# State-space parameters beside the first layer: loads on GpSimd's queue, later stores, one table per piece, zeros stored first

## The chip, the cores and the metric

The kernel runs on one core of one Trainium2 chip. The metric is the device time of one execution in microseconds; lower is better. TensorE is the engine for matrix products, VectorE, ScalarE and GpSimd are the engines for elementwise work, and SyncE only issues transfers. In the rows of the profile they are PE (PEld is its weight load), DVE, ACT, POOL and SP; ACTq and SPq are transfers issued from ScalarE's and SyncE's queues.

## The reference

A network of four layers over 512 tokens and 2048 channels in float32: "ab" (gated linear attention and forgetting attention), "c" (a state space layer, S5), then an even and an odd layer. Each ends with a projection added to its input. What the change touches is the preparation of layer c's parameters, which depend on the weights alone:

```python
step = jnp.exp(log_step)[:, None]
mag = jnp.exp(lr * step)
lb_re, lb_im = mag * jnp.cos(li * step), mag * jnp.sin(li * step)
den = lr * lr + li * li
nr, ni = lb_re - 1.0, lb_im
coef_re = (nr * lr + ni * li) / den
coef_im = (ni * lr - nr * li) / den
bb_re = coef_re[..., None] * b_re - coef_im[..., None] * b_im
bb_im = coef_re[..., None] * b_im + coef_im[..., None] * b_re
...
# x_t = Lbar x_{t-1} + Bbar u_t ; y_t = Re(C x_t) + D u_t
```

Groups of 16 channels share a state of 64 complex numbers. The kernel evaluates the recurrence in chunks, so it needs tables of powers of Lbar, and products of B and C with such powers.

## The kernel before

Every large product is taken over float32 values that are split in a high and a low part, with three matmuls for each product of two values. A weight tile of 128 x 512 is loaded by SyncE's queue into `wraw` (3 buffers); ScalarE writes its high part and VectorE its low part into `whl` (4 buffers); TensorE then does 12 matmuls of 512 columns with it, into `pj`. This repeats all through the kernel: one tile after another, with the attention, gates and norms of the layers in between. So ScalarE and VectorE have to be in time with one split each per tile.

The parameters of layer c are made beside layer ab. `emit` defines `params(o)`, and layer ab calls it as `beside(o)` at 21 places ("pieces"): 0 before the forgetting attention, 1 to 8 in its loop, 9 to 12 after the gates, 13 to 20 behind the chunks of the first `w_out` (line 480). Piece 0 is `s5_params`: chains of small rows on GpSimd that make the powers and store them per batch in DRAM (`s5tab`, lines 988 to 992), and `s5w`. There are 16 batches of S5 groups, and for each of them two more things are made:

- `s5_tables`, two batches in each of the pieces 1 to 8: a load of `lm` from `s5tab` (line 1004), four multiplications and two sums on VectorE (`cst`, `acc`, `hc`), and two stores on ScalarE's queue (lines 1020 and 1021).
- `s5_batch_params`, one batch in each of the pieces 3 to 18: loads of `smb`, `s5_bc` and `s5w` on SyncE's queue (lines 1032, 1040, 1041), a scale of -C on ScalarE (line 1043), products on GpSimd into two `hc` tiles that are cleared first and stored (lines 1052 and 1060), GG on VectorE (six rows, `vs` and `acc`) with a store on ScalarE, and BB on GpSimd (`fac`). At the next piece the second half follows: 16 small matmuls into `tr`, placed behind the last matmul so far (`net.last`), X3 from them, and four small stores (line 1093).

The order of the instructions on each engine comes from a planner that puts rows where it expects their inputs to be ready; `after(...)` puts a row behind a given one. Each engine works its rows in order. A tag of tiles has a fixed number of buffers: `acc`, `cst`, `fac` and `lm` have one, `hc` and `vs` four, `rawb` eight. A row that needs a buffer waits until the earlier user of it is done. `acc` is also the sum of squares that `w_out` gathers for the next norm.

## Time and profile before

| | |
|---|---|
| median of 3 runs | 3410.19 us (3409.04 to 3414.12) |
| the profiled execution | 3407.61 us |
| its span, first to last instruction | 3405.8 us |
| mean granted clock of TensorE | 0.994 |
| GpSimd busy | 23 % of the span |
| transfers | 390 MB |

The profile is of one execution. Its span leaves 1.8 us outside. The granted clock is a share of full speed. The rows below are its views: the page, tables by windows of time, sums of waits, groups of equal instructions, and the timeline.

### The profile page before, as it was taken

What the parts mean: (1) busy time and instruction counts of PE and PEld (TensorE: products, weight loads), DVE (VectorE), ACT (ScalarE), POOL (GpSimd) and SP (SyncE); (2) the same over time, 40 slices, a digit from 0 to 9 for tenths busy, and PEclk for the clock granted to TensorE, in tenths of its full rate; (3) what the DMA queues carried; (4) which work ended last, traced back from release to release, by engine and by line L of the source; (5) the groups of instructions that cost most, each with busy time, mean ns of one, the idle gap of its engine ahead of it and who ended that gap; (6) DMA issues with size and microseconds to landing.
All of it is one profiled execution on the core that took longest, in us unless ns stands there. A gap on an engine that the chain in (4) does not pass through costs nothing.

```text
span 3405.8 us, 45778 instructions
## 1 busy us (share of the span) xinstructions
PE 3349.1 (98%) x16332; PEld 2722.4 (80%) x16332; DVE 1907.8 (56%) x3213; ACT 1337.7 (39%) x2497; POOL 784.1 (23%) x974
## 2 busy tenths in 40 slices
PE   9999999999999999999999999999999999999997
PEld 8888776777788888888888777888888788888885
DVE  5753457787556576834354655453544545647634
ACT  5443432233343333423343655232433444535532
POOL 0330364348602223200221100012110120212011
PEclk9999999999999999999999999999999999999999
DMA  5223335576634444343443223334333223332343
GB/s 156 72 69 91 87 109 159 169 218 207 206 107 132 135 144 141 116 121 118 145 127 90 66 75 90 94 120 145 105 92 81 73 65 81 80 88 75 106 120 106
DMA packets 389013, 390.01 MB, mean 115 GB/s; under 512 B 66968, under 2 KB 327448, under 8 KB 388784
## 3 DMA queue, kind: packets, MB, share of 16 engines
q1 hardware_dynamic: 362992, 354.64, 36.4%
q10 hardware_dynamic: 22464, 22.12, 1.9%
q0 software_dynamic: 3328, 10.32, 0.8%
q8 instruction: 128, 2.10, 0.3%
q14 instruction: 101, 0.83, 0.1%
HBM read 340.71 MB, written 46.25 MB: 114 GB/s over the span
## 4 chain that ended last, share of the span: by engine, by line
PE 73%; DVE 2%; POOL 1%; issue 1%; DMA 0%; DVEq 0%; ACT 0%; SPq 0%
PE pj L152 66%; PE sc L152 3%; PE po L152 3%; PE tr L156 1%; POOL wt L140 1%; DVE wk L140 0%; PE tr L152 0%; DVE hl L140 0%; DMA vs<-s5w 0%; DVE wk L1139 0%; DVE whl L140 0%; POOL cst L140 0%; DVE ha L143 0%; DVE sc L140 0%; DVE hc L143 0%
## 5 line engine op out<-in xcount | busy, mean ns | idle before, releaser
L152 PE MATMUL pj<-hl,whl 128*128 128x512 f32 x10224 | 2459.6, 398 | 14.8 <-DVE whl L140 7.3
L152 PEld LDWEIGHTS pj<-hl,whl 128*128 128x128 f32 x10224 | 1912.8, 189 | 456.3 <-DVE whl L140 10.2
L140 DVE TENSOR_TENSOR whl<-wraw,whl 128x512 fp32r<-128x512 f32 (+2 forms) x1064 | 805.3, 759 | 1082.7 <-ACT whl L137 1077.5
L137 ACT ACTIVATE whl<-wraw 128x512 fp32r<-128x512 f32 (+2 forms) x1064 | 661.5, 623 | 1353.9 <-PE pj L152 1096.6
L152 PE MATMUL pj<-whl,hl 128*128 128x512 f32 (+2 forms) x2112 | 466.1, 380 | 4.1 <-DVE whl L140 2.3
L152 PEld LDWEIGHTS pj<-whl,hl 128*128 128x128 f32 x2112 | 375.4, 191 | 81.4 <-DVE whl L140 3.1
L140 POOL TENSOR_TENSOR acc<-acc,wt 128x512 f32<-128x512 f32 x73 | 102.7, 1415 | 798.7 <-ACT wt L137 797.4
L137 ACT ACTIVATE wk<-sc,sm 128x256 f32<-128x256 f32 (+3 forms) x160 | 79.6, 502 | 90.3 <-DVE sm L148 86.8
L140 POOL TENSOR_TENSOR ha<-wk,ha 64x512 fp32r<-64x512 f32 x32 | 45.0, 1407 | 290.7 <-ACT ha L137 264.2
L140 POOL TENSOR_TENSOR wt<-wt,acc 64x508 f32<-64x508 f32 x32 | 63.9, 1995 | 181.4 <-DVE wt L140 125.7
L140 POOL TENSOR_TENSOR wt<-ha,wk 128x256 f32<-128x256 f32 x72 | 61.9, 888 | 127.4 <-PE sc L152 66.9
L152 PE MATMUL po<-pt,vs 128*128 128x128 f32 x560 | 80.0, 276 | 0.2
L152 PEld LDWEIGHTS po<-pt,vs 128*128 128x128 f32 x560 | 72.8, 192 | 3.2 <-ACT pt L137 0.8
L152 PE MATMUL sc<-ha,ha 128*128 128x128 f32 (+1 forms) x224 | 71.2, 390 | 3.5 <-DVE ha L140 2.7
L156 PE MATMUL tr<-ident,wk 128*128 128x128 f32 x416 | 71.4, 275 | 1.4 <-DVE pt L509 1.1
L137 ACT ACTIVATE pt<-tr 128x384 f32<-128x384 f32 (+3 forms) x96 | 46.7, 486 | 62.0 <-PE tr L156 60.1
L148 DVE TENSOR_SCALAR wk<-wk,sm 128x256 f32<-128x256 f32 (+3 forms) x160 | 65.4, 422 | 4.5
L140 POOL TENSOR_TENSOR fac<-wt,acc 128x512 fp32r<-128x512 f32 x8 | 10.8, 1353 | 244.3 <-ACT acc L137 130.3
L156 PEld LDWEIGHTS tr<-ident,wk 128*128 128x128 f32 x416 | 52.0, 141 | 18.8 <-issue 3.4
L137 ACT ACTIVATE ge<-ge 128x512 f32<-128x512 f32 x64 | 40.3, 630 | 66.7 <-DVE ge L140 55.7
L521 DVE TENSOR_REDUCE sm<-sc 128x1 f32<-128x128 f32 (+3 forms) x96 | 45.8, 487 | 34.1 <-PE sc L152 33.5
L140 POOL TENSOR_TENSOR cst<-vs,vs 128x256 f32<-128x256 f32 x64 | 53.5, 855 | 32.1 <-DMA vs<-s5w 18.8
(316 smaller groups left out, 2984.3 us busy)
## 6 DMA issues: line engine op xcount, KB each, us to landing
wraw<-in_l_w_in_dram SPq DMA_DIRECT2D x272, 256.0 KB, 2.8
wraw<-in_ab_w_in_dram SPq DMA_DIRECT2D x216, 256.0 KB, 2.8
wraw<-in_c_w_in_dram SPq DMA_DIRECT2D x128, 256.0 KB, 2.7
wraw<-in_l_w_out_dram SPq DMA_DIRECT2D x128, 256.0 KB, 2.9
wraw<-in_ab_w_out_dram SPq DMA_DIRECT2D x64, 256.0 KB, 3.4
wraw<-in_glu_w_dram SPq DMA_DIRECT2D x64, 256.0 KB, 2.9
wraw<-in_c_w_out_dram SPq DMA_DIRECT2D x64, 256.0 KB, 3.0
wraw<-in_l_w_in_dram SPq DMA_DIRECT2D x128, 128.0 KB, 2.3
```

The costliest lines, as they stand in the source:

```text
L137: return self.nc.scalar.activation(out, in_, func, **kw)
L140: return (eng or self.nc.vector).tensor_tensor(out, a, b, op=op)
L148: return e.tensor_scalar(out, a, s1, None, op0=op0)
L152: return self.nc.tensor.matmul(out, l, r, start=start, stop=stop)
L156: return self.nc.tensor.transpose(out, in_, self.ident[:k, :k])
L521: self.nc.vector.tensor_reduce(mx, pb[:, 0:w], axis=AX.X, op=ALU.max)
```

## The change

It moves and re-cuts the making of the parameters; what is computed stays the same.

- The loads of `s5_tables` and `s5_batch_params` go from SyncE's queue to GpSimd's. `s5_bc` is loaded in two parts, the part with C into a tile that all batches share by halves (`small`).
- `s5_tables` makes one batch per piece, in pieces 1 to 16, each of its rows behind VectorE's last two-operand row so far (`last_dve`). Its stores come a piece later, behind ScalarE's last row so far (`last_act`).
- The store of GG, and those of X3, come a piece later than their data.
- The products of B are no longer put into cleared tiles. `s5_clear`, in pieces 0 to 3, stores zeros over the whole of the 16 targets in DRAM (16 stores of 512 KB on ScalarE's queue), and each batch stores its 128-partition product in two strided stores of 512 pieces of 256 B (GpSimd's queue). 
- The scale of -C goes from ScalarE to GpSimd, a copy of X3 from ScalarE to VectorE.
- Other buffers: the power tables in `rawb` in place of `vs`, `wrow` in `lm` in place of `ha`, BB in two halves of one `fac` tile, GG in turn in `acc2` and `hc`, the products in `bc`.

```diff
     def act(self, out, in_, func=AF.Copy, **kw):
-        return self.nc.scalar.activation(out, in_, func, **kw)
+        self.last_act = self.nc.scalar.activation(out, in_, func, **kw)
+        return self.last_act
...
-    def s5_tables(self, b0):
+    def s5_tables(self, b):
...
-        tab = self.t("lm", [P, S])[:, 0:384].rearrange("p (b f) -> p b f", b=2)
-        self.dma.dma_start(tab, self.s5tab[b0:b0 + 2, :, 0:192].rearrange("b p f -> p b f"))
-        for b in range(2):
...
+        tab = self.t("lm", [P, S])
+        nc.gpsimd.dma_start(tab[:, 0:192], self.s5tab[b][:, 0:192])
...
+        with self.after([self.last_dve]):
             self.tt(v4(u[0]), av(0), bv(0), A.mult)
...
-            d = self.dp.tile([P, 2, S], F32, name=self.name("s5ph"))
+        yield
+        d = self.dp.tile([P, 2, S], F32, name=self.name("s5ph"))
+        with self.after([self.last_act]):
             nc.scalar.dma_start(d[:, 0], C)
             nc.scalar.dma_start(d[:, 1], Sn)
...
     def s5_batch_params(self, b):
...
-        self.dma.dma_start(M, self.s5tab[b][:, 196:236])
+        if b == 0:
+            self.s5bb = self.t("fac", [P, 2, 2, 4, 32])
+            self.s5small = self.t("hc", [P, 2, 256])
+        BB, small = self.s5bb[:, b % 2], self.s5small[:, b % 2]
+        CP, X3 = small[:, 0:128].rearrange("p (i q c) -> p i q c", i=2, q=4), small[:, 128:240]
+        g.dma_start(M, self.s5tab[b][:, 196:236])
...
-        self.dma.dma_start(X1[:, 0:896], I["s5_bc"][b])
-        self.dma.dma_start(Y[:, 0:512],
-                           self.wtab[b].rearrange("g s i q p -> (g s) (i q p)").unsqueeze(1).to_broadcast([8, 16, 512]))
-        self.act(X1[:, 320:384], X1[:, 320:384], scale=-1.0)
+        g.dma_start(X1[:, 0:768], I["s5_bc"][b][:, 0:768])
+        g.dma_start(small[:, 0:128], I["s5_bc"][b][:, 768:896])
+        g.dma_start(Y[:, 0:512],
+                    self.wtab[b].rearrange("g s i q p -> (g s) (i q p)").unsqueeze(1).to_broadcast([8, 16, 512]))
+        self.ts(small[:, 64:128], small[:, 64:128], -1.0, eng=g)
+        g.memset(X3[:, 0:48], 0.0)
...
         for i in range(2):
-            o = self.hd("hc")
-            g.memset(o, 0.0)
-            self.tt(z0, BT[:, 0], WT[:, i], A.mult, eng=g)
+            self.tt(o[:, i], BT[:, 0], WT[:, i], A.mult, eng=g)
             self.tt(z1, BT[:, 1], WT[:, 1 - i], A.mult, eng=g)
-            for gg in range(2):
-                r = slice(64 * gg, 64 * gg + 64)
-                self.tt(o[r].rearrange("p (q g f) -> p q g f", q=4, g=2)[:, :, gg],
-                        z0[r].rearrange("p (q f) -> p q f", q=4), z1[r].rearrange("p (q f) -> p q f", q=4),
-                        A.add if i else A.subtract, eng=g)
-            g.dma_start(d[1][:, i], o)
+            self.tt(o[:, i], o[:, i], z1, A.add if i else A.subtract, eng=g)
+        for gg in range(2):
+            r = slice(64 * gg, 64 * gg + 64)
+            g.dma_start(d[1][r].rearrange("p i (q g f) -> p (i q) g f", q=4, g=2)[:, :, gg],
+                        o[r].rearrange("p i (q f) -> p (i q) f", q=4))
...
+    def s5_clear(self, batches):
+
+        zero = self.t("rawb", [P, S])
+        self.nc.gpsimd.memset(zero, 0.0)
+        for b in batches:
+            d = [self.dp.tile(sh, F32, name=self.name("s5d")) for sh in ([P, 2, 256], [P, 2, S], [4, P, 64])]
+            self.s5d.append(d)
+            with self.after([self.last_act]):
+                self.nc.scalar.dma_start(d[1], zero.unsqueeze(1).to_broadcast([P, 2, S]))
...
             if o == 0:
                 net.s5_params()
-            elif o <= 8:
-                net.s5_tables(2 * (o - 1))
-            for b in pending:
-                with net.after([net.last]):
-                    next(b, None)
-            pending.clear()
+            if o < 4:
+                net.s5_clear(range(4 * o, 4 * o + 4))
+            for b in list(pending):
+                if next(b, b) is b:
+                    pending.remove(b)
+            if 1 <= o <= 16:
+                pending.append(net.s5_tables(o - 1))
+                next(pending[-1])
             if 3 <= o < 19:
                 pending.append(net.s5_batch_params(o - 3))
-                next(pending[0])
+                next(pending[-1])
```

What this does to the order of the rows on two engines is seen at three places. `whl` is a weight split; the numbers are those of the tiles. The code's lines are moved by the change: line 1020 of before is 1029, 140 is 142, 143 is 148.

First place: ScalarE's order in the forgetting attention, with the phase table stores (lines 1020 and 1021, `s5ph`), a store's data being VectorE's `hc`. Before:

```order
L137 ACTIVATE rawb_4220<-po_4209 128x512
L137 ACTIVATE whl_4637<-wraw_4635 128x512
L1020 DMA s5ph_4058<-hc_4048 128x512
L137 ACTIVATE vs_4252<-vs_4252 128x64
L137 ACTIVATE whl_4654<-wraw_4652 128x512
L1021 DMA s5ph_4058<-hc_4049 128x512
L137 ACTIVATE whl_4671<-wraw_4669 128x512
L1020 DMA s5ph_4071<-hc_4061 128x512
L137 ACTIVATE whl_4688<-wraw_4686 128x512
L1021 DMA s5ph_4071<-hc_4062 128x512
```

In the change, at the same head's end:

```order
L138 ACTIVATE rawb_4279<-po_4268 128x512
L1029 DMA s5ph_4299<-hc_4123 128x512
L1118 DMA s5d_4284<-rawb_4281 256x1x512
L1118 DMA s5d_4288<-rawb_4281 256x1x512
L1118 DMA s5d_4292<-rawb_4281 256x1x512
L138 ACTIVATE whl_4711<-wraw_4709 128x512
L1118 DMA s5d_4296<-rawb_4281 256x1x512
L1030 DMA s5ph_4299<-hc_4124 128x512
L138 ACTIVATE whl_4728<-wraw_4726 128x512
L138 ACTIVATE whl_4745<-wraw_4743 128x512
```

The stores between weight splits have become those of the table of a piece before (`hc_4123` beside piece tiles numbered over 4270), and the zero stores (line 1118) stand among them.

Second place: VectorE's order in the gates, from the 226th weight tile to the 227th or 228th; `lm` is a table's load, `ge` a gate, `hl` the split of `w_out`'s input. Before:

```order
L140 TENSOR_TENSOR whl_6863<-wraw_6861,whl_6863 128x512
L143 SCALAR_TENSOR_TENSOR vs_6162<-own,cols,tr_6350 128x16
L140 TENSOR_TENSOR whl_6880<-wraw_6878,whl_6880 128x512
L140 TENSOR_TENSOR acc_6399<-vs_6377 128x256
L140 TENSOR_TENSOR ge_6760<-pj_6628,bc_230 128x512
L140 TENSOR_TENSOR vs_6377<-vs_6376,smb_6374 128x256 x2
L140 TENSOR_TENSOR acc_6399<-vs_6377 128x256
L140 TENSOR_TENSOR vs_6591<-vs_6590,smb_6588 128x256 x2
L140 TENSOR_TENSOR whl_6897<-wraw_6895,whl_6897 128x512
```

In the change:

```order
L142 TENSOR_TENSOR whl_6824<-wraw_6822,whl_6824 128x512
L142 TENSOR_TENSOR hc_6103<-cst_6104,acc_6105 128x512
L142 TENSOR_TENSOR hc_6130<-vs_6115 128x256
L148 SCALAR_TENSOR_TENSOR rawb_4279<-ge_6509,rawb_4279 128x512
L142 TENSOR_TENSOR acc_6350<-vs_6335 128x256
L142 TENSOR_TENSOR whl_6841<-wraw_6839,whl_6841 128x512
L142 TENSOR_TENSOR vs_6115<-hc_4316,smb_6112 128x256 x2
L142 TENSOR_TENSOR ge_6715<-pj_6583,bc_230 128x512
L142 TENSOR_TENSOR cst_6324<-lm_6320 128x512
L142 TENSOR_TENSOR acc_6325<-lm_6320 128x512
L142 TENSOR_TENSOR hc_6130<-vs_6115 128x256
L142 TENSOR_TENSOR whl_6858<-wraw_6856,whl_6858 128x512
```

Table rows (`cst`, `acc` from `lm`, and `hc`) now stand between the weight splits here, beside GG's rows; before, all tables were done by this place.

Third place: VectorE's order in the first tiles of layer c, the 305th to the 307th. Before, three weight splits stood in a row (`whl_8988`, `whl_9005`, `whl_9022`), with nothing between them up to the 313th:

```order
L140 TENSOR_TENSOR whl_8988<-wraw_8986,whl_8988 128x512
L140 TENSOR_TENSOR whl_9005<-wraw_9003,whl_9005 128x512
L140 TENSOR_TENSOR whl_9022<-wraw_9020,whl_9022 128x512
L140 TENSOR_TENSOR whl_9039<-wraw_9037,whl_9039 128x512
L140 TENSOR_TENSOR whl_9056<-wraw_9054,whl_9056 128x512
```

In the change:

```order
L142 TENSOR_TENSOR whl_8968<-wraw_8966,whl_8968 128x512
L142 TENSOR_TENSOR hc_7481<-cst_7483,acc_7484 128x512
L142 TENSOR_TENSOR cst_7483<-lm_7479 128x512
L142 TENSOR_TENSOR acc_7484<-lm_7479 128x512
L142 TENSOR_TENSOR whl_8985<-wraw_8983,whl_8985 128x512
L142 TENSOR_TENSOR hc_7482<-cst_7483,acc_7484 128x512
L142 TENSOR_TENSOR hc_7509<-vs_7494 128x256
L142 TENSOR_TENSOR vs_7494<-hc_4316,smb_7491 128x256 x2
L142 TENSOR_TENSOR hc_7509<-vs_7494 128x256
L142 TENSOR_TENSOR whl_9002<-wraw_9000,whl_9002 128x512
```

The tables of the last batches stand here, behind the norm that frees `acc`, and the rows of GG that go with them.

## Rows read from the trace of the kernel before

**Rows 1.** The page's first part: busy us (share of the span) x instructions, by engine.

```profile
PE 3349.1 (98%) x16332; PEld 2722.4 (80%) x16332; DVE 1907.8 (56%) x3213; ACT 1337.7 (39%) x2497; POOL 784.1 (23%) x974
```

**Rows 2.** Windows: stretch, length, busy PE, PEld, DVE, ACT, POOL, clock, DMA share, GB/s.

```profile
500.00:550.00 50.00, 39.63 (x148) 29.42 (x148) 41.80 (x53) 8.44 (x16) 38.79 (x89) 0.86 0.61 180
...
660.00:700.00 40.00, 36.55 (x188) 27.81 (x187) 35.56 (x69) 10.87 (x27) 21.80 (x31) 0.96 0.76 212
...
760.00:810.00 50.00, 41.74 (x249) 31.28 (x248) 47.46 (x62) 16.91 (x35) 43.67 (x63) 0.93 0.55 171
```

**Rows 3.** Waits of TensorE, 420 to 1000: total us, times, longest.

```profile
PE pj L152 <- DVE whl L140: 9.6, 7, 3.6
PE tr L152 <- POOL fac L140: 7.0, 5, 5.4
```

**Rows 4.** Waits of ScalarE, 500 to 560 us.

```profile
ACT whl L137 <- DVE hc L140: 29.7, 9, 5.7
```

**Rows 5.** Timeline, 500 to 526: start, us, instruction, idle before and its releaser.

```profile
505.74 0.33 ACTq L1021 DMA_DIRECT2D s5ph<-hc  x1
...
506.19 0.63 ACT L137 ACTIVATE whl<-wraw 128x512 fp32r<-128x512 f32 x1 [5.66 <-DVE hc L140]
...
509.37 1.06 DVE L140 TENSOR_TENSOR cst<-lm 128x512 f32<-128x512 f32 x1 [3.66 <-DMA lm<-s5tab]
...
512.07 13.16 PE L152 MATMUL pj<-hl,whl 128*128 128x512 f32 x48 [3.58 <-DVE whl L140]
```

**Rows 6.** Chain of waits, 770 to 802: start, us, what.

```profile
793.10 3.97 DMA vs<-s5w
...
800.47 0.44 PE tr L152 x24
```

**Rows 7.** Waits of SyncE's queue, 440 to 900 us.

```profile
SPq L1041 <- DVE acc L140: 19.5, 8, 4.3
```

**Rows 8.** Groups of VectorE, 440 to 1000: busy us, mean ns, idle before.

```profile
L140 DVE TENSOR_TENSOR whl<-wraw,whl 128x512 fp32r<-128x512 f32 x170 | 140.4, 831 | 114.0 <-ACT whl L137 113.5
L140 DVE TENSOR_TENSOR vs<-vs,smb 128x256 f32<-128x256 f32 x64 | 42.9, 708 | 6.3 <-POOL cst L140 2.0 <-POOL wt L988 1.8 <-DMA s5d<-vs 1.4
...
L140 DVE TENSOR_TENSOR cst<-lm 128x512 f32<-128x512 f32 x32 | 35.2, 1099 | 19.3 <-DMA lm<-s5tab 10.9 <-POOL hc L140 8.3
L140 DVE TENSOR_TENSOR hc<-cst,acc 128x512 f32<-128x512 f32 x32 | 22.2, 694 | 0.5
L140 DVE TENSOR_TENSOR acc<-vs 128x256 f32<-128x256 f32 x32 | 20.0, 624 | 1.7 <-DMA s5d<-acc 1.3
...
L140 DVE TENSOR_TENSOR hl<-rawb,hl 128x512 fp32r<-128x512 f32 x8 | 6.4, 822 | 1.8 <-ACT hl L137 1.8
```

**Rows 9.** TensorE's `pj` matmuls alone in a full stretch: busy us, count, clock.

```profile
850.00:1000.00 150.00, 146.55 (x621) 1.00 0.53 165
```

**Rows 10.** Groups of GpSimd, 440 to 1000.

```profile
L140 POOL TENSOR_TENSOR hc<-cst 64x256 f32<-64x256 f32 x64 | 56.5, 883 | 3.5
L140 POOL TENSOR_TENSOR cst<-vs,vs 128x256 f32<-128x256 f32 x64 | 53.5, 855 | 32.1 <-DMA vs<-s5w 18.8 <-DVE sm L148 5.9 <-DVE hc L140 4.0
...
L1060 POOL DMA_DIRECT2D s5d<-hc x32 | 18.6, 580 | 4.5 <-POOL hc L140 4.5
L1052 POOL MEMSET hc<- 128x512 f32 x32 | 16.7, 525 | 40.0 <-DMA s5ph<-hc 19.2 <-DMA s5d<-hc 9.0 <-DVE sm L530 7.6
```

**Rows 11.** Timeline of GpSimd and VectorE, 499 to 513.

```profile
500.49 1.13 DVE L140 TENSOR_TENSOR acc<-lm 128x512 f32<-128x512 f32 x1
...
500.63 1.08 POOL L989 COPY wt<-hc 128x32 f32<-128x32 f32 x1
...
502.40 1.07 POOL L992 DMA_DIRECT2D s5tab<-wt  x2
...
502.93 1.07 DVE L140 TENSOR_TENSOR cst<-lm 128x512 f32<-128x512 f32 x1
...
505.80 0.21 POOL L989 COPY wt<-hc 128x32 f32<-128x32 f32 x1
```

More of the change, by code (lines that the diff above doesn't have):

```diff
@@ L112, in __init__ @@
         self.dma = nc.sync
+        self.s5d = []
         self.setup()
@@ L946, in s5_params @@
         cmul(N[11], N[12], c2, d2, c2, d2)
-        Tb = [self.t("vs", [P, 16, H]) for _ in range(2)]
+        half = lambda: self.hd("rawb").rearrange("p (n h) -> p n h", h=H)
+        Tb, Tb2 = [half(), half()], [half(), half()]
         Ta = [self.t("hc", [P, 8, H]) for _ in range(2)]
@@ L1080, in s5_batch_params @@
+            self.tt(v1, BP[:, 1], co(1 - i), A.mult, eng=g)
+            self.tt(BB[:, i], v0, v1, A.add if i else A.subtract, eng=g)
         yield
+        with self.after([self.last_act]):
+            nc.scalar.dma_start(d[0], GG)
         pt = self.ps("tr")
         rows = lambda q: slice(32 * q, 32 * q + 32)
-        for i in range(2):
-            for q in range(4):
-                self.mm(pt[rows(q), 0:16], BB[:, i, q], CP[:, i, q], start=(i == 0), stop=(i == 1))
-        for i in range(2):
-            for q in range(4):
-                self.mm(pt[rows(q), 16:64], BB[:, i, q], GG[:, i, q * 64:q * 64 + 48], start=(i == 0), stop=(i == 1))
@@ L1089, in s5_batch_params @@
-        g.memset(X3[:, 0:48], 0.0)
-        self.stt(X3[:, 48:64], self.own, self.c("s5_d", b), pt[:, 0:16], A.mult, A.add)
-        self.act(X3[:, 64:112], pt[:, 16:64])
-        for s_ in range(4):
-            nc.scalar.dma_start(d[2][s_], X3[:, 48 - 16 * s_:112 - 16 * s_])
+        with self.after([self.last]):
+            for i in range(2):
+                for q in range(4):
+                    self.mm(pt[rows(q), 0:16], BB[:, i, q], CP[:, i, q], start=(i == 0), stop=(i == 1))
+            for i in range(2):
+                for q in range(4):
+                    self.mm(pt[rows(q), 16:64], BB[:, i, q], GG[:, i, q * 64:q * 64 + 48], start=(i == 0), stop=(i == 1))
@@ new lines, in s5_batch_params @@
+        with self.after([self.last_dve]):
+            self.stt(X3[:, 48:64], self.own, self.c("s5_d", b), pt[:, 0:16], A.mult, A.add)
+            nc.vector.tensor_copy(X3[:, 64:112], pt[:, 16:64])
+        yield
+        with self.after([self.last_act]):
+            for s_ in range(4):
+                nc.scalar.dma_start(d[2][s_], X3[:, 48 - 16 * s_:112 - 16 * s_])
+    def s5_clear(self, batches):
[4 more added lines that the diff above has]
+            self.s5d.append(d)
+            with self.after([self.last_act]):
+                self.nc.scalar.dma_start(d[1], zero.unsqueeze(1).to_broadcast([P, 2, S]))
@@ L1610, in emit @@
                 net.s5_params()
+                net.s5_clear(range(16))
                 for b in range(16):
-                    if b % 2 == 0:
-                        net.s5_tables(b)
+                    for _ in net.s5_tables(b):
+                        pass
                     for _ in net.s5_batch_params(b):
```

58 lines of the change are left out of this document (29 added, 29 removed).

## The prediction

> **What bounds the kernel now.** I read the page's busy times first: TensorE is busy for 98 per cent of a span of 3405.8 us [rows 1], so a change can only move the few stretches in which TensorE stands still or runs at a lower clock. The table by windows shows where these lie: in 420 to 1000 us, where the S5 parameters are made beside the first layer, there are three. Stage A, 500 to 550 us, has 39.63 us of TensorE in 50 at a granted clock of 0.86; stage B, 660 to 700, has 36.55 in 40 at 0.96; stage C, 760 to 810, has 41.74 in 50 at 0.93 [rows 2]. So 10.4, 3.5 and 8.3 us are idle. A granted clock under 1.00 is a mixture of the levels 2.4 and 1.2 GHz, and the three stretches that idle are the three with a lower one; what it costs is busy time by what is missing to 1.00: 5.5, 1.5 and 2.9 us. All that these parameters cost today is thus 15.9 + 5.0 + 11.2 = **32 us**. No edit to them can give more.
>
> The waits then say who ended the idling. TensorE's two largest are for VectorE's low half of a weight tile (9.6 us) and for GpSimd's `fac` (7.0) [rows 3]. They are two mechanisms. In stage A, ScalarE waited 29.7 us in nine pieces for VectorE's `hc` ahead of a weight split [rows 4]. The timeline shows one: the store of a phase table (L1021) is issued at 505.74, just after VectorE made it, and the weight split behind it on ScalarE's queue had stood 5.66 us. VectorE itself then waits 3.66 us for the next table's load, with a weight split behind that row, and TensorE starts 3.58 us late at 512.07 [rows 5]. In stage C it is the chain of a batch: a load of 3.97 us, GpSimd's multiplications, its `fac`, and only then TensorE's small matmuls [rows 6].
>
> **The change, part by part.** *Stage A.* The stores move a piece later, so their data are old when ScalarE comes to them (the order's first place). One table per piece, not two, halves VectorE's burst. Also SyncE no longer stands in front of the weights with parameter loads: its largest such stand, L1041 for VectorE's `acc`, is 19.5 us [rows 7]. I take the whole 15.9 us as gone. Bounds: 12 if the tables still left there cost the 3.66 us of one load wait, 15.9 if not.
>
> *Stage B.* Nothing new stands there and VectorE does less; I take the 5.0 as gone; bounds 0 and 5.0.
>
> *Stage C.* The batch chain's cost, 11.2 us, goes only if nothing takes its place. But a table per piece takes sixteen pieces, and the gates and the first w_out chunks now carry them. I count VectorE's rows in the new order between the 221st and the 248th weight tile: 23 table multiplications at 1.099 us (25.3), 12 table sums at 0.694 (8.3), 22 and 10 for GG at 0.708 and 0.624 (15.6 and 6.2), 28 weight splits at 0.831 (23.3) and 32 rows of gates and `hl` splits, all taken at the 0.822 of `hl` (26.3): **105 us** [rows 8]. TensorE has 28 tiles of 12 matmuls there. A stretch with nothing between them has 621 in 146.55 us [rows 9], so 0.236 each and 79 us. Before, the same tiles had no table rows: 23.3 + 17.0 + 7.5 for GG + 24.7 for 30 others = 72 us, under TensorE's 79. The excess of 26 us is softened by the four `whl` buffers, 4 x 12 x 0.236 = 11.3 us of lead if they are full. So about 14.5 us idle. With the clock on top, which cost 0.53 us per idle us in stage A and 0.35 in C, I take 0.44: **+21**. Bounds: 9 if gaps elsewhere on VectorE's list let it catch up by a further 5 us and the clock holds; 26 x 1.53 = 40 if no lead exists.
>
> *Start of layer C.* The table's `acc` has one buffer, which w_out's sum of squares holds until the norm. So the tables of the last batches leave w_out and stand in layer C's first tiles (the order's third place). Between tiles 302 and 316, VectorE has 15 splits (12.5), 15 multiplications (16.5), 8 sums (5.6), 14 and 8 for GG (9.9 and 5.0) and 2 rows of the norm (1.6): 51 us, against 182 matmuls, 43 us; before, 14 us. The excess is 8. Bounds: 0 with the lead full, 8 x 1.53 = 12 with none. I take the middle, **+6**: the rows just ahead are the `hl` splits, which leave little lead.
>
> *Zeros.* Sixteen stores of 512 KB stand in ScalarE's order, behind GpSimd's memsets. The trace has no such wait. The lower bound is 0, since a full lead covers three tiles, 8.5 us. The upper is stage A's, a ScalarE wait of 5.66 us that made TensorE 3.58 us late, for two of them: 7. I take **+2**, nearer to 0, because the memsets need only `rawb`.
>
> *GpSimd.* Its queue gets five load issues per batch: 80 at 0.580 us (a batch's store; 46 us). It loses 32 memsets at 0.525 (17) and 64 half adds at 0.883 (57), and gets 32 full ones at 0.855 (27) [rows 10]: about 0 in sum. The two stores of 512 short pieces have no row; I take the 0.580 of a store of 128 rows as the lower bound and four times that as the upper, 1.7 us more each, and take the lower. The scale of -C and the copy of X3 change engines; they are one short row each per batch, beside TensorE's tiles, and without that cover 16 times no more than the 0.21 to 1.08 us of a small copy [rows 11]. The zeros' 8 MB go beside the weights, at DMA shares of 0.55 to 0.76 [rows 2], and I cost them at nothing; if the weights came late by them, it would show as ScalarE waiting for `wraw`.
>
> Here the trace speaks on GpSimd and VectorE together: a 32-column copy took 1.08 us beside a table row of VectorE and 0.21 without one, while a pair of DMA issues took 1.07 us beside such a row [rows 11]. So copies are held and issues are not; the sum goes by the rows, with 0.58 us per issue, and an issue that is held as the copy was is a rival below. The Trainium skill (SBUF — State Buffer, section "SBUF: two separate sides", the box on DMAs issued from GpSimd) says that VectorE can lock GpSimd out of a port pair that they share, that a DMA on GpSimd's queue then can't get its descriptors, and that ScalarE's or SyncE's queue should be taken instead; it gives about 0.62 us alone and 3.1 us overlapped. By it, as an estimate from that page, the 80 loads would take up to 2.5 us more each, 200 us of GpSimd's time, and the sum would be that of the rival or worse. The copies here agree with it, the issue rows do not.
>
> *Sum:* -15.9 - 5.0 - 11.2 + 21 + 6 + 2 = -3, so 3407.6 becomes about 3405 for an execution like the profiled one. That one lies 2.6 us under the median of the runs shown, 3410.19. So **3407 us**. About 0.2 per cent, 6.8 us, is what a measurement of this kernel can tell from no change.
>
> **Rivals.** *All hidden.* VectorE's list has gaps that my count does not see (it idles in 44 per cent of the span [rows 1]), the lead stays and the new rows cost a few us. Stages A to C give back 32 less up to 9, so -23 to -32: 3378 to 3387, say 3384. For it: before, tables beside attention cost nothing outside three stretches. Against it: the 105 against 79.
>
> *Slower, VectorE binds twice.* It is the mechanism of stage C without a lead, and layer C's likewise: -32 + 40 + 12 + 2 = +22, so 3432. It decides when VectorE's rows per tile stay above TensorE's 2.83 us for longer than four tiles; for it, stage A lost 10.4 us in just such a stretch [rows 2]; against it, part of that came from ScalarE's stores, which are mended, and VectorE's list there had the load wait besides.
>
> *Slower, GpSimd's queue is late.* If each of a batch's seven or eight issues is held for a table row, 1.1 us, then GpSimd needs 8 us more per batch; its chain already ended the wait in stage C [rows 6]. The four batches whose tables stand in layer C's first tiles have 43 us there; 32 us late there, less the lead of 11, with the clock 30: 3407.6 + 30 + 2.6 = 3440. The equal 1.07 us of issues speak against it [rows 11]. By that page's rule it would be the likeliest.
>
> *Not done as said:* if the stores still stood ahead of their data, nothing would change in stage A: 3410 + 13 = 3423; the order excludes it for the rows shown.
>
> **Numbers.** Forecast (the costs move from stages A and B to stage C and layer C, 3397 to 3417): 0.45. All hidden: 0.26. VectorE twice: 0.20, with the undone case. GpSimd's queue: 0.09. The forecast's own spread lies by 0.10 below and 0.05 above the 0.2 per cent. So faster 0.36, the same 0.30, slower 0.34. The range leaves out the worst of the slower cases and the last of the hidden one: 3380 to 3434.
>
> **What would show it.** Right: no ScalarE wait for `hc` ahead of a weight split near 500 to 560 us and that stretch full; TensorE waiting for VectorE's `whl` near 770 to 830, with VectorE at ten tenths; tables' rows beside layer C's first matmuls. Wrong: stage A still with waits, stage C full in spite of the tables (all hidden), VectorE waiting for `lm` while GpSimd's issues last longer than 0.6 us (its queue), or a wait of ScalarE for `rawb` near 400 or 450.

## The result and the profile after

| | before | after |
|---|---|---|
| median | 3410.89 us (4 runs) | 3435.2 us (3430.44 to 3436.57, 4 runs) |
| the profiled execution, its span | 3407.61, 3405.8 us | 3430.44, 3428.6 us |
| mean granted clock of TensorE | 0.994 | 0.993 |

The ratio is 1.0069, 95% interval [1.0057, 1.0081]: slower, by 0.7 per cent. The forecast was 3407 in 3380 to 3434; the median lies 1.2 us over the range, next to the rival in which VectorE binds twice (3432). The profiled execution of the changed kernel is the fastest of its four, 4.8 us under their median.

The table by windows of the changed kernel, columns as in [rows 2], shows where the idling went:

```profile
380.00:420.00 40.00, 35.66 (x156) 26.19 (x156) 25.65 (x58) 12.72 (x30) 37.49 (x71) 1.00 0.49 151
...
460.00:500.00 40.00, 37.80 (x179) 29.39 (x178) 24.52 (x59) 15.25 (x36) 22.01 (x56) 1.00 0.65 202
500.00:550.00 50.00, 50.00 (x229) 40.94 (x229) 16.80 (x27) 12.33 (x20) 3.08 (x7) 1.00 0.48 145
...
660.00:700.00 40.00, 40.00 (x190) 31.72 (x189) 30.74 (x78) 15.04 (x35) 15.67 (x23) 1.00 0.63 173
700.00:760.00 60.00, 55.83 (x333) 44.13 (x332) 39.52 (x58) 18.02 (x31) 31.38 (x35) 0.97 0.61 177
760.00:810.00 50.00, 39.90 (x209) 29.09 (x207) 42.68 (x61) 13.62 (x24) 42.41 (x44) 0.93 0.50 145
810.00:830.00 20.00, 11.61 (x72) 8.79 (x72) 13.61 (x20) 2.30 (x4) 18.06 (x28) 0.74 0.61 164
830.00:900.00 70.00, 66.39 (x349) 52.78 (x350) 42.02 (x55) 19.34 (x31) 48.42 (x69) 0.98 0.71 217
...
1000.00:1040.00 40.00, 33.23 (x205) 25.11 (x204) 31.50 (x51) 5.58 (x9) 25.43 (x34) 0.91 0.63 180
1040.00:1100.00 60.00, 57.28 (x343) 47.04 (x342) 37.57 (x62) 24.13 (x47) 22.40 (x32) 1.00 0.47 137
```

Stages A and B of [rows 2] are full. In 700 to 900 us TensorE now idles for 4.2, 10.1, 8.4 and 3.6 us; with the clock's share (busy time by what is missing to 1.00: 1.7, 2.8, 3.0, 1.3) that is 35 us. Layer C's start loses 12: 6.8 idle and 3.0 of clock to 1040, then 2.7 idle where the kernel before had 0.4. And 4.3 and 2.2 us are new at 380 to 420 and 460 to 500. The stretches in which TensorE had idled again have the lower clocks: 0.74 at 810 to 830, between the levels of 2.4 and 1.2 GHz.

TensorE's waits, 380 to 1100 us, which answer to [rows 3]:

```profile
PE pj L157 <- DVE hl L142: 9.3, 1, 9.3
PE pj L157 <- DVE whl L142: 9.1, 6, 4.3
PE tr L157 <- DVE hc L142: 7.7, 5, 2.7
PE tr L157 <- DVE hc L1104: 5.5, 2, 4.4
```

The four largest are all for VectorE. ScalarE's wait for `hc` at 500 to 560 [rows 4] is gone; its largest wait there is now for TensorE:

```profile
ACT whl L138 <- PE pj L157: 38.2, 18, 5.4
```

The longest wait of TensorE is the one to read. The timeline of the changed kernel, rows of GpSimd, VectorE and TensorE:

```profile
797.12 10.16 POOL L142 TENSOR_TENSOR vs<-vs,vs 128x256 f32<-128x256 f32 x1
807.24 0.74 POOL L142 TENSOR_TENSOR bc<-vs,vs 128x256 f32<-128x256 f32 x1
...
796.47 0.69 DVE L142 TENSOR_TENSOR ge<-pj,bc 128x512 f32<-128x512 f32 x1
797.07 1.08 DVE L142 TENSOR_TENSOR cst<-lm 128x512 f32<-128x512 f32 x1
...
805.61 1.06 DVE L142 TENSOR_TENSOR acc<-lm 128x512 f32<-128x512 f32 x1
815.36 0.47 DVE L142 TENSOR_TENSOR vs<-hc,smb 128x256 f32<-128x256 f32 x1 [8.69 <-POOL fac L142]
...
817.50 4.71 PE L157 MATMUL pj<-hl,whl 128*128 128x512 f32 x13 [9.26 <-DVE hl L142]
```

A GpSimd product that took 0.86 us on average before [rows 10] lasts 10.16 us. From 797.07 to 806.67 VectorE works without a pause, on rows that take both operands from SBUF; GpSimd's row ends 0.6 us after VectorE stops. The rest of GpSimd's batch (the next product takes 0.74) then comes late, VectorE stands 8.69 us for it with weight splits behind the waiting row, and TensorE idles 9.26 us. By these times VectorE first keeps GpSimd out, and then waits for what it kept back.

VectorE's two largest waits of this kind at 700 to 900 us; in the kernel before, none for GpSimd or for a load is over 1.3 us there:

```profile
DVE vs L142 <- DMA hc<-in_s_bc_dram: 9.6, 3, 4.6
DVE vs L142 <- POOL fac L142: 8.7, 1, 8.7
```

The row that waited 8.69 us reads C from `hc`. GpSimd issued a load of C at 813.08, after the held product, and such a load lands 2.2 us later in the median, so at about 815.3. Whether `fac` or that load let the row go can't be told from this; both stand behind the held product in GpSimd's order.

Groups of GpSimd, 400 to 1050 us, against [rows 10]:

```profile
L142 POOL TENSOR_TENSOR vs<-vs,vs 128x256 f32<-128x256 f32 x32 | 45.0, 1407 | 0.5
L142 POOL TENSOR_TENSOR bc<-vs,vs 128x256 f32<-128x256 f32 x32 | 36.2, 1133 | 30.2 <-DMA vs<-s5w 25.4 <-issue 3.8 <-DMA s5d<-bc 1.0
...
L1071 POOL DMA_DIRECT2D s5d<-bc x32 | 22.4, 708 | 3.9 <-POOL bc L142 2.6 <-issue 1.1 <-POOL hc L1059 0.2
...
L1011 POOL DMA_DIRECT2D lm<-s5tab x16 | 9.2, 577 | 68.0 <-DVE acc L142 66.0 <-DVE tk L142 2.0
```

The issues are near the forecast's 0.58 us: 0.577 for a table's load and 0.708 for a store in short pieces. The products, 64 of them at 0.855 before, now cost 1.407 and 1.133.

### The profile page after: what moved, and what is told of

It is laid out like the page before. It is cut to its first block, busy times and chain, and to the rows that moved or that the text cites. A ratio compares the mean times of both kernels' runs of the same rounds, so it can differ in the third digit from the quotient of the medians.

```text
span 3428.6 us, 45810 instructions
## 1 busy us (share of the span) xinstructions
PE 3352.5 (98%) x16332; PEld 2720.7 (79%) x16332; DVE 1895.7 (55%) x3229; ACT 1334.1 (39%) x2465; POOL 824.6 (24%) x1042
## 4 chain that ended last, share of the span: by engine, by line
PE 88%; POOL 5%; DVE 3%; DMA 2%; issue 1%; ACT 0%; DVEq 0%; ACTq 0%; SPq 0%; POOLq 0%
PE pj L157 78%; PE sc L157 5%; PE po L157 3%; PE tr L161 1%; POOL vs L142 1%; POOL wt L142 1%; PE tr L157 1%; POOL fac L142 1%; DMA vs<-s5w 0%; DVE whl L142 0%; DVE hl L142 0%; DVE acc L142 0%; POOL acc L142 0%; DMA lm<-s5tab 0%; DVE wk L142 0%
## 5 line engine op out<-in xcount | busy, mean ns | idle before, releaser
L148 DVE SCALAR_TENSOR_TENSOR ge<-ge,ge 128x512 f32<-128x512 f32 x60 | 48.9, 816 | 19.5 <-ACT ge L138 19.3
```

The source lines that it names most:

```text
L148: return self.nc.vector.scalar_tensor_tensor(out, a, s, b, op0=op0, op1=op1, **kw)
```

## The experiments

Each kernel is the changed one with the edit shown, unless it says otherwise; times stand beside the kernel before on the same chip. The loss of the change is 0.69 per cent (ratio 1.0069).

### What it is not: the queue of the loads, the zeros

**e2_loads_sp**

```diff
-        nc.gpsimd.dma_start(tab[:, 0:192], self.s5tab[b][:, 0:192])
+        self.dma.dma_start(tab[:, 0:192], self.s5tab[b][:, 0:192])
...
-        g.dma_start(M, self.s5tab[b][:, 196:236])
+        self.dma.dma_start(M, self.s5tab[b][:, 196:236])
```

(and the three others of a batch.)

> The change with one part undone: the five loads of a batch (table, smb, two of s5_bc, s5w) are issued from SyncE's queue again; tables, stores and zeros stay as changed. Theory A expects no large move, 3427 to 3440, with long rows on GpSimd near 750 and 800 still there. Theory B expects most of the loss back, 3400 to 3415.

3429.88 us, ratio 1.0059 [1.0046, 1.0073]. The loads' queue comes out at 0.1 per cent, which the intervals do not tell from nothing. Long GpSimd products stay: the longest lasts 7.9 us. In the windows of the one profiled execution two moves offset each other: 700 to 900 loses 28 us where the changed kernel loses 35, and 460 to 500 loses 8.9 where it loses 2.2.

**e3_zeros_first**

```diff
-            if o < 4:
-                net.s5_clear(range(4 * o, 4 * o + 4))
...
+            net.s5_clear(range(16))
             h = net.layer_ab(raws, beside=params if "c" in layers else None)
```

> The change with the 16 zero stores moved to the start of the kernel, ahead of layer ab, in place of pieces 0 to 3. If the zeros and their memsets cost the 6.5 us of idle TensorE in 380 to 420 and 460 to 500, 3426 to 3431; if that idling is of GpSimd's power chains and not of the zeros, 3433 to 3437. Theories A and B say the same of the rest: 700 to 900 stays as it is.

3446.3 us, 1.0108 [1.0094, 1.0122], above both ranges: in 0 to 100 us TensorE is busy for 83.26 us, where the kernel before has 93.70. But the idling that the edit was to remove is still there, 3.6 of the 4.3 us at 380 to 420, so most of it isn't the zeros':

```profile
380.00:420.00 40.00, 36.43 (x159) 27.17 (x157) 22.97 (x39) 10.15 (x20) 37.24 (x76) 1.00 0.30 82
```

### The price of the late tables

**e1_tables_two**: two tables in each of the pieces 1 to 8 again, with their stores in the same piece.

```diff
-            if 1 <= o <= 16:
-                pending.append(net.s5_tables(o - 1))
-                next(pending[-1])
+            if 1 <= o <= 8:
+                for b in (2 * o - 2, 2 * o - 1):
+                    for _ in net.s5_tables(b):
+                        pass
```

> The change with one part undone: two tables per piece in pieces 1 to 8 with their stores in the same piece, as before; loads on GpSimd's queue, zeros first and the late stores of GG and X3 stay. Theory A (the tables that moved into the gates and the first w_out chunks and into layer C keep VectorE without a gap; GpSimd, which shares a port with it, stands, and VectorE and TensorE then wait for GpSimd) expects the 35 us of 700 to 900 and the 12 us of layer C's start nearly gone, and some 10 us of stage A back: 3393 to 3410. Theory B (the parameter loads come late from GpSimd's queue, wherever the tables stand) expects little: 3422 to 3436.

3415.76 us, 1.0018 [1.001, 1.0027]: three quarters of the loss come back. The median is 6 us over the first range: 460 to 500 now holds only 33.12 us of TensorE at 0.91, and 760 to 810 still 39.59.

**e4_own_u**: the last four tables take a buffer of `ha` for their second product, not `acc`.

```diff
-        u = [self.t("cst", [P, S]), self.t("acc", [P, S])]
+        u = [self.t("cst", [P, S]), self.t("ha" if b >= 12 else "acc", [P, S])]
```

> The change with one buffer moved: for the batches 12 to 15 the second factor of a table is put in a tile of ha in place of acc, so these tables no longer wait for the norm of layer C and stand in w_out. Theory A expects the 12 us of layer C's start gone, since VectorE has room in the later w_out chunks: 3420 to 3427. Theory B expects them to come back in w_out, or to stay: 3431 to 3438.

3430.55 us, 1.0063 [1.0051, 1.0076]. `acc` is what held these tables back, since layer C's start is now full; but their cost moves to 830 to 1000, where the changed kernel lost 5 us and this one 15. That is what theory B said:

```profile
830.00:900.00 70.00, 64.94 (x367) 50.83 (x368) 57.40 (x77) 16.85 (x27) 58.45 (x75) 0.95 0.68 208
900.00:1000.00 100.00, 96.58 (x491) 76.23 (x490) 60.47 (x93) 45.40 (x64) 40.80 (x53) 0.97 0.66 197
1000.00:1040.00 40.00, 40.00 (x174) 32.79 (x173) 12.71 (x20) 10.91 (x20) 1.45 (x4) 1.00 0.34 100
```

**e12_six_tables**

```diff
+        if b >= 6:
+            yield
+            self.s5ph.append(self.s5ph[b - 6])
+            return
         tab = self.t("lm", [P, S])
```

> The changed kernel that leaves out the last ten of the sixteen phase tables (their loads, rows and stores; ten batches use the tables of others). All else stands: GpSimd's products, GG, the zeros. Theory A, the tables' own rows on VectorE are what 700 to 900 us (35 us) and the start of layer C (11.7 us) cost: 700 to 830 and 1000 to 1040 idle for under 10 us together, and the time is 3388 to 3405. Theory B, the batch chain (GpSimd's products, GG, BB, the small matmuls), crowded as it is, costs the most of it, as in the kernel before at 760 to 810: 3412 to 3425.

3389.92 us, 0.9956 [0.9942, 0.9969]. From 1.0069 that is 1.1 per cent, 38 us, for ten tables; the edit takes out their loads and stores with their rows, so this is the price of the whole table. The stretches fill up, GpSimd's products are short (0.742 us in the median of `vs<-vs,vs`), and 700 to 900 loses 10 us in all. That is theory A:

```profile
760.00:810.00 50.00, 45.85 (x282) 35.55 (x281) 37.15 (x56) 14.91 (x26) 41.25 (x59) 1.00 0.55 168
810.00:830.00 20.00, 20.00 (x114) 15.73 (x115) 13.93 (x19) 6.21 (x10) 17.48 (x29) 1.00 0.75 236
830.00:900.00 70.00, 69.11 (x386) 55.04 (x384) 42.36 (x62) 19.25 (x32) 47.51 (x76) 1.00 0.65 198
```

### VectorE keeps GpSimd out

**m1_ports** leaves out the network. It runs rows of VectorE beside four GpSimd products of 128x256:

```python
def two(n):
    for i in range(n):
        net.lastv = v.tensor_tensor(dst[i % 3], a, b, op=A.mult)
def psum(n):
    for i in range(n):
        net.lastv = v.tensor_tensor(dst[i % 3], ps, b, op=A.mult)
...
two(16); pool(4); sync(); psum(16); pool(4)
```

> A kernel of its own that leaves out the whole network: GpSimd does 4 products of 128x256 alone, then beside 16 rows of VectorE with both operands in SBUF, 16 with one operand in PSUM, 16 with one operand and a scalar; then one store of 256 KB and one load of 256 KB from GpSimd's queue, beside 16 two-operand rows and without. Theory A (the shared port) expects 0.72 us for GpSimd's product alone and beside the PSUM rows, and one product that lasts as long as VectorE's row of two-operand instructions, some 9 to 10 us. Theory B expects GpSimd's products unchanged, under 1.3 us everywhere, and the issue of the transfers beside VectorE's rows to take 3 us or more in place of 0.6.

In its timeline a product takes 0.72 us alone. Beside rows with two operands from SBUF both engines slow down:

```profile
9.52 0.72 POOL L1629 TENSOR_TENSOR hb<-hb,hb 128x256 f32<-128x256 f32 x1
...
10.81 4.11 POOL L1629 TENSOR_TENSOR hb<-hb,hb 128x256 f32<-128x256 f32 x4
10.96 7.51 DVE L1633 TENSOR_TENSOR rawb<-rawa,rawa 128x512 f32<-128x512 f32 x9
```

They take turns, 1.05 us a product and 1.21 us a VectorE row. Beside rows with one operand in PSUM both run at full speed (four products in 3.1 us); beside rows with one operand and a scalar four took 3.5 us. A DMA issue beside the dense rows takes 0.81 or 0.59 us (a store, a load), alone 0.69 or 0.55: not held. The one long product that theory A expected did not come.

**m2_late**: as m1, but the product becomes ready while 24 such rows run back to back.

```python
for i in range(24):
    d = t4 if i == 4 else dst[i % 3]
    net.lastv = v.tensor_tensor(d, a, b, op=A.mult)
    if i == 4:
        g.tensor_tensor(po, t4[:, 0:256], pb, op=A.add)
        for _ in range(2):
            g.tensor_tensor(po, pa, pb, op=A.add)
```

> A second kernel of its own that leaves out the network: VectorE does 24 rows with both operands in SBUF, back to back, and GpSimd's three products become ready only after the fourth of them, so that VectorE holds the port when GpSimd comes. Then the same with the 13th row reading PSUM; then with GpSimd ready after the first row; then a store from GpSimd's queue, ready after the fourth. If whoever comes second to a busy port stands until VectorE leaves it: the first product lasts some 12 us, to VectorE's end, in the first part, and to the 13th row in the second. If the two take turns, as in m1_ports: 0.7 to 1.3 us everywhere and VectorE's rows up to 1.2 us.

Still turns of 1.03 to 1.05 us. So "dense VectorE rows shut GpSimd out" is refuted as a general rule, although the changed kernel shows it. From the part in which the 13th row reads PSUM:

```profile
27.69 1.04 POOL L1653 TENSOR_TENSOR hb<-ha,hb 128x256 f32<-128x256 f32 x1 [2.88 <-DVE ha L1648]
```

**e10_gaps**: behind each table row a memset of 128x16 on VectorE, which reads nothing.

```diff
+        self.gap = self.cp.tile([P, 16], F32, name="gap")
...
+                r_ = self.tt(o_, x, y, op)
+                with self.after([r_]):
+                    nc.vector.memset(self.gap, 0.0)
```

> The changed kernel with one small memset of 128x16 on VectorE behind each of the 96 table rows; a memset reads nothing, so it breaks up VectorE's dense stretches of rows with two operands. Theory A, the GpSimd rows that lasted 10.16 and 7.25 us in the changed kernel are kept out by those stretches, and what is lost at 810 to 820 us (VectorE 8.69 us for fac, TensorE 9.26 us idle, then the lower clock) hangs on them: no GpSimd product over 3.5 us, the 8.69 us wait under 3 us, and 10 to 20 us come back, 3415 to 3425. Theory B, VectorE has too much to do there and GpSimd only shows it: 96 rows of some 0.1 us more, no gain, 3432 to 3442, whatever becomes of GpSimd's rows.

3424.68 us, 1.0049 [1.0035, 1.0063]: 96 rows of 0.07 us more, and the kernel is some 7 us faster by the ratios, whose intervals overlap a little; theory A had 10 to 20. The product of 10.16 us and the wait of 8.69 are gone. Groups by tile of this kernel, ns as min/median/max:

```profile
L142 POOL TENSOR_TENSOR vs<-vs,vs x32: 714/878/1581, 460.7 to 1039.3; 128x256 f32<-128x256 f32 x32
L142 POOL TENSOR_TENSOR bc<-bc,vs x32: 716/740/3519, 463.2 to 1040.1; 128x256 f32<-128x256 f32 x32
```

The one long product left shows how such a stand ends, in the timeline of this kernel:

```profile
773.84 3.52 POOL L142 TENSOR_TENSOR bc<-bc,vs 128x256 f32<-128x256 f32 x1
...
776.07 0.69 DVE L148 SCALAR_TENSOR_TENSOR rawb<-ge,rawb 128x512 f32<-128x512 f32 x1
776.69 1.22 DVE L142 TENSOR_TENSOR hl<-rawb,hl 128x512 fp32r<-128x512 f32 x1
776.71 0.07 DVE L1025 MEMSET gap<- 128x16 f32 x1
```

It ends 0.65 us after the memset, about a product's own length, and the VectorE row beside its end lasts 1.22 us where its neighbours last 0.69. What is left is load: VectorE is busy for 50.00 us in 760 to 810, and 700 to 900 still loses 30 us of the 35:

```profile
760.00:810.00 50.00, 41.98 (x221) 31.12 (x220) 50.00 (x78) 14.76 (x25) 38.50 (x50) 0.93 0.53 150
810.00:830.00 20.00, 13.10 (x109) 9.40 (x108) 19.46 (x40) 3.79 (x6) 16.41 (x23) 0.84 0.74 218
```

**e11_all_gaps**: the same memsets in e7_all (below).

> The version that tied with the kernel before (two tables per piece, loads on SyncE, zeros on GpSimd, powers in vs), with the same memsets behind the table rows. It had GpSimd products of 7.4, 6.8 and 13.2 us in a row from 750 to 777 us. Theory A: they fall under 3.5 us and the time to 3395 to 3405, under the kernel before. Theory B: 3407 to 3414, the same as without the memsets.

3411.66 us, 1.0011 [1.0003, 1.002], where e7_all has 0.9999. The products of 7.4, 6.8 and 13.2 us are gone here too, and nothing is gained: 700 to 900 loses 21 us, against 20 in e7_all. Yet in e7_all too VectorE stood behind the held products, until GpSimd's scale of -C, and TensorE idled 7.05 us with it:

```profile
783.43 0.94 DVE L142 TENSOR_TENSOR vs<-hc,smb 128x256 f32<-128x256 f32 x1 [7.13 <-POOL hc L153]
```

With the memsets that wait is gone, and the loss stands elsewhere: 760 to 830 loses 7 us less than in e7_all, and 700 to 760 and 830 to 900 lose 9 more. One thing works against the edit in both kernels: when GpSimd gets in, VectorE's rows last longer. The multiplications of GG at 700 to 900 go from 0.600 to 0.818 us in e10_gaps, and from 0.565 to 0.728 here. So what a held product costs by itself is not shown: letting it in gained some 7 us in one kernel and nothing in the other.

### What stage A hung on

**b1_ph_pool**: the kernel before, its phase table stores on GpSimd's queue.

```diff
-            nc.scalar.dma_start(d[:, 0], C)
-            nc.scalar.dma_start(d[:, 1], Sn)
+            nc.gpsimd.dma_start(d[:, 0], C)
+            nc.gpsimd.dma_start(d[:, 1], Sn)
```

> The kernel before with one edit: the stores of the phase tables go on GpSimd's queue in place of ScalarE's. It tests the reading of stage A alone. If ScalarE's standing in front of these stores made the 10 us of idle in 500 to 550: 3395 to 3404. If VectorE's two tables per piece made it: 3406 to 3413.

3409.1 us, 1.0003 [0.9994, 1.0012]. No wait of ScalarE for `hc` is left at 500 to 560. Stage A loses 11.1 us in place of 15.9 [rows 2], ScalarE waits for `wraw` in place of `hc`, and 810 to 830, full before, loses 5.2, so the time is the same. The prediction's first reason for stage A, the stores, was a symptom for the most part. More of the cause comes out below, with e15_ten_six_vs.

```profile
500.00:550.00 50.00, 41.83 (x172) 32.12 (x170) 42.72 (x52) 8.73 (x15) 45.78 (x93) 0.93 0.59 178
...
ACT whl L137 <- DMA wraw<-in_ab_w_in_dram: 17.0, 7, 4.0
```

### Other mixtures of the parts

All four have two tables per piece, as e1_tables_two. **e5_two_sp** has the loads on SyncE's queue besides; **e6_two_zg** the zeros on GpSimd's queue (`nc.gpsimd.dma_start(d[1], zero...)`); **e7_all** both, and the power tables in `vs` again; **e9_half_pool** is e7_all with every second table's rows on GpSimd (`self.tt(..., eng=net.nc.gpsimd)`).

> Tables two per piece in pieces 1 to 8 as in e1_tables_two, and in addition the five loads of a batch on SyncE's queue. e1 left 10.4 us of TensorE idle in 760 to 810, with VectorE waiting 9.7 us for a load of C. If those are GpSimd's late issues: 3400 to 3409. If the loads' place does not matter: 3413 to 3418.

3417.45 us, 1.0024 [1.0015, 1.0034]: no better than e1.

> e1_tables_two with the 16 zero stores on GpSimd's queue behind their memsets, in place of ScalarE's. e1 has ScalarE waiting 7.6 us for a memset and 7.3 for GpSimd near 460 to 500, where TensorE idles 6.9 us and loses 3.6 to the clock. If the zeros on ScalarE's queue cause it: 3404 to 3410. If not: 3413 to 3419.

3414.96 us, 1.0016 [1.0007, 1.0025]: no gain by the zeros' queue.

> Tables two per piece, loads on SyncE's queue, zero stores on GpSimd's, and the power tables in vs again, so that GpSimd's chains of powers start as late as before. What is left of the change are the late stores of GG and X3, the zeros and the full-width products. If each of the parts undone costs what the windows say (35 + 12 for the tables, 6.5 for zeros and power chains, some 5 for the loads), the sum is at or under before: 3393 to 3408. If the rest of the change costs something of its own, above 3412.

3408.67 us, 0.9999 [0.999, 1.0008]: ties with the kernel before, and lies 0.7 over the first range. Which of its three edits does this is not shown: the first two gain nothing one at a time, and the third was not run alone with two tables per piece.

> e7_all with every second table made on GpSimd in place of VectorE. VectorE's dense stretches shorten by 46 us in sum, GpSimd gets some 8 x 9 = 70 us. If VectorE's density is what costs in e7: 3393 to 3405. If GpSimd's products and table rows then are late themselves: 3410 to 3425.

3414.6 us, 1.0021 [1.0012, 1.003]: the tables on GpSimd crowd the batch chain; 760 to 810 has 33.71 us of TensorE.

### The tables elsewhere

**e13_ten_six** and **e14_twelve_four** (two tables in each of the pieces 1 to 6, one in 17 to 20): the late ones as in e4_own_u, and, in e13,

```diff
-            if 1 <= o <= 16:
-                pending.append(net.s5_tables(o - 1))
+            for b in {1: (0, 1), 2: (2, 3), 3: (4, 5), 4: (6, 7), 5: (8,), 6: (9,),
+                      15: (10,), 16: (11,), 17: (12,), 18: (13,), 19: (14,), 20: (15,)}.get(o, ()):
+                pending.append(net.s5_tables(b))
```

> The changed kernel with ten tables in pieces 1 to 6 (two each in 1 to 4) and six in pieces 15 to 20, none between, the late ones' second product in a buffer of ha. So no table row stands between the 206th and the 259th weight tile, nor in layer C. Theory A, what a table costs depends on what VectorE has beside it: with attention at 500 to 700 and the later w_out chunks at 900 to 1000 (VectorE busy for 49 to 54 us in 100 there) it is mostly hidden; 3395 to 3407, under the kernel before. Theory B, the rows cost wherever they are put, 40 us for ten: 3408 to 3425.

> As e13_ten_six, with twelve tables in pieces 1 to 6 (two each) and four in pieces 17 to 20. Theory A: 3393 to 3407; if it is slower than the other by more than 5 us, two tables per piece beside attention are what costs, if faster by that, the late ones. Theory B: 3408 to 3425.

e13: 3404.76 us, 0.9988 [0.9979, 0.9997], so 0.12 per cent under the kernel before, with an interval that ends just below 1; e14: 3412.88, 1.0016 [1.0007, 1.0025]. By its expectation's own rule, the 8 us between the two are the price of two more tables in pieces 5 and 6. Sixteen tables in e13's places cost 0.3 per cent over e12's 0.9956, 11 us in place of 38, so the price belongs to the place. No GpSimd product of 128x256 lasts over 1.6 us there. Its windows:

```profile
460.00:500.00 40.00, 34.80 (x159) 26.53 (x158) 27.40 (x63) 15.39 (x36) 22.27 (x72) 0.91 0.71 217
500.00:550.00 50.00, 50.00 (x229) 40.87 (x228) 22.76 (x32) 12.44 (x20) 1.60 (x3) 1.00 0.53 167
...
760.00:810.00 50.00, 47.40 (x295) 36.56 (x295) 44.11 (x63) 18.19 (x32) 40.22 (x61) 1.00 0.50 151
810.00:830.00 20.00, 20.00 (x138) 15.63 (x138) 15.58 (x22) 6.22 (x10) 17.25 (x28) 1.00 0.70 220
830.00:900.00 70.00, 70.00 (x392) 55.71 (x389) 55.19 (x71) 20.08 (x33) 59.04 (x84) 1.00 0.72 220
900.00:1000.00 100.00, 99.09 (x477) 79.00 (x476) 74.94 (x102) 45.28 (x64) 20.28 (x26) 0.98 0.63 191
```

VectorE does 20 us more in 900 to 1000 than in the changed kernel, at a cost to TensorE of 3 us.

**e15_ten_six_vs**: e13 with the power tables in `vs` again.

```diff
-        half = lambda: self.hd("rawb").rearrange("p (n h) -> p n h", h=H)
-        Tb, Tb2 = [half(), half()], [half(), half()]
+        whole = [self.t("vs", [P, 16, H]) for _ in range(2)]
+        Tb, Tb2 = [x[:, 0:8] for x in whole], [x[:, 8:16] for x in whole]
```

> e13_ten_six with the power tables in vs again, as in the kernel before, where GpSimd's chain of powers waits for those buffers until 443.8 us. The changed kernel and e13_ten_six make that chain from 380 us on, beside TensorE's idling of 4.4 us at 380 to 420 and of 2.2 and 5.2 us at 460 to 500 (the term for the zeros, 2 forecast, 6.5 measured). Theory A, that idling hangs on the chain's early place: 380 to 500 is full and 3392 to 3400. Theory B, the tables then begin 12 weight tiles later and crowd 500 to 600, as in the kernel before: 380 to 500 is full, 500 to 600 loses as much or more, 3401 to 3413.

3405.65 us, 0.9992 [0.9983, 1.0001]: theory B. The two kernels differ in nothing but the buffers of the powers, and what e13 loses at 380 to 500 (4.4 idle, then 5.2 and 3.1 of clock) stands for the most part at 500 to 600 here (11.2, clock included). GpSimd's busy time moves along with it: 0.00 us at 380 to 420, where the changed kernel has 37.49, and 39.63 at 500 to 550, where the changed kernel has 3.08 and the kernel before 38.79 [rows 2]:

```profile
380.00:420.00 40.00, 40.00 (x188) 31.54 (x187) 20.38 (x60) 15.00 (x35) 0.00 (x0) 1.00 0.53 155
...
460.00:500.00 40.00, 38.70 (x195) 31.34 (x194) 28.34 (x49) 13.60 (x30) 31.97 (x67) 1.00 0.39 104
500.00:550.00 50.00, 41.67 (x176) 32.12 (x175) 34.40 (x44) 9.68 (x16) 39.63 (x96) 0.98 0.57 179
```

## Why the prediction was wrong

The mechanism of the forecast was right in the main (the costs move from stages A and B to stage C and to layer C); three terms were too small, all on the same side.

| term | forecast (bounds) | measured |
|---|---|---|
| stage A | -15.9 (12 to 15.9) | -15.9 |
| stage B | -5.0 (0 to 5.0) | -5.0 |
| stage C and the first chunks | -11.2 + 21 (9 to 40) | -11.2 + 35 |
| start of layer C | +6 (0 to 12) | +12 |
| zeros, 380 to 500 | +2 (0 to 7) | +6.5, of the chain of powers |
| sum | -3 | +21 (spans: +22.8) |

- **Stages A and B** came out to the tenth because both stretches came out full, but A not for the first reason given, so its size is partly luck. Stores that don't wait give back 4.8 of its 15.9 us (b1_ph_pool), and with two tables per piece it is full (e1_tables_two, 50.00 us). It hangs on the chain of powers: with its old buffers the chain works at 500 to 550 and TensorE has 41.67 us there, with the new ones it is done before and the stage is full (e15 against e13). One table per piece, the second reason, seems to count as well: with the early chain and two tables per piece 460 to 500 loses 9.9 us (e1) and 8.3 (e13), with one table 2.2. No run has one table per piece and the old buffers.
- **Stage C, the step that failed: the full lead, and GpSimd at nothing.** The count of rows, 105 us of VectorE against 79 of TensorE, pointed to the right stretch, and the runs put 38 us on the ten late tables (e12_six_tables). Too small was the loss per excess: the term took 26 us less a full lead of 11.3 and came to +21; it measured +35, near the bound of 40 that has no lead. So the lead was next to nothing, or something else cost as much; why is shown in part. The step "GpSimd (...) about 0 in sum" took GpSimd's products at their old 0.855 us. In the dense stretch they last up to 10.16, and VectorE waits 8.69 behind one; it is busy for 42.68 of 50 us and then 13.61 of 20, not at the ten tenths that the prediction named as its sign. With the memsets of e10_gaps that wait is gone, VectorE is at ten tenths, and 700 to 900 still loses 30 us. By these windows some 5 of the 14 us by which the term was short go with the held products, and 9 are lost without them. As the memsets also make VectorE's own rows longer, and gain nothing in e11_all_gaps, this split is an estimate and not shown; no run measures the lead itself.
- **The evidence was there and was put to one side.** In [rows 11] a GpSimd copy took 1.08 us beside a table row and 0.21 without one, and the text said that copies are held. That price went to two small rows of a batch and not to the 64 products, GpSimd rows that read SBUF as the copy does.
- **Layer C** measured the upper bound, the one without any lead; the middle had been taken.
- **Zeros.** Most of the idling isn't theirs (e3_zeros_first, e15_ten_six_vs). It is the price of moving the chain of powers forward: "Other buffers" of the change, which the prediction did not cost at all, and which also emptied stage A.
- **The rival of GpSimd's queue** had the right engine and the wrong row: issues, at 577 to 708 ns, were not held; products were. The issues were late all the same where they stood behind a held product in GpSimd's order, but with the loads on SyncE's queue the time is nearly the same (e2_loads_sp). The Trainium skill (SBUF — State Buffer, section "Who interferes with whom") says that a VectorE row with two SBUF inputs contends with GpSimd rows that read SBUF, and infers that it leaves the issuing of DMAs alone. The traces agree with both parts: 0.72 against 1.05 us for a product in m1_ports, 0.59 to 0.81 for an issue beside such rows and 0.55 to 0.69 without them. So the prediction's estimate of up to 2.5 us more for each load did not follow from that page of the Trainium skill for the rows that fill VectorE here, which have two SBUF inputs.
- **The range** ended 1.2 us short. It took the bounds of the terms one at a time; those of stage C and layer C both rest on VectorE's lead and fell together, and the case of that, "VectorE binds twice", had 0.20. The last step out of the range is chance: the sum adds 2.6 us from the profiled execution to the median, and the changed kernel's median lies 4.8 us over its own.

**Open:** why VectorE keeps GpSimd out for ten rows and more in the changed kernel, and takes turns with it in m1_ports and m2_late, at the same shapes and with both operands in SBUF. Those two kernels repeat one VectorE row, with TensorE and ScalarE at rest; the network's mixture of rows, its strided table operands and its other traffic were not tried there. The Trainium skill (SBUF — State Buffer, section "SBUF: two separate sides") says that whoever starts first holds the shared ports for its whole row; that would give turns, as in the two small kernels, and not a product that waits through fifteen rows. The long products begin within 0.1 us after a VectorE row's start in most cases (797.12 after 797.07), but not in all. What stood at their ends was seen: a VectorE row with an operand in PSUM (`ge<-pj` from 756.67, the product of 7.25 us ending at 757.36), a pause of VectorE (from 806.67, ending at 807.28), or a row that reads nothing (e10_gaps).

## What to carry to other kernels

Work that is moved away from a crowded stretch costs by what the engine does where it lands: ten tables cost 38 us in pieces 7 to 16, among the gates, the first `w_out` chunks and the start of layer C, and sixteen tables without those places cost only 11 us more than six. So make the count of rows per tile for the new place, and look for the stretch that has room (VectorE busy for half) before choosing one. Where VectorE gets dense with rows that have two SBUF operands, take GpSimd's rows at the duration seen beside such rows, not at their mean, and ask who waits for GpSimd's last row; but don't count on a gain from letting GpSimd in, as VectorE's rows then last longer. Terms of a sum that rest on one lead are one term: they are right or wrong together.
